# A seventh seven-product pair in the second column pair of the second MLP product

## The chip, the cores and the metric

The kernel runs on one core of a Trainium2 chip. The metric is device time in microseconds (us) of one execution of the whole program; a lower time is better. The kernel before takes 2110.73 us (median of three runs, 2110.59 to 2112.64).

## The reference

Four pre-norm residual layers share one residual stream `x` of 256 tokens by 2048 features, in fp32. Two of them mix tokens (one with latent attention and a matrix memory, one with dilated attention), and each of these is followed by a squared-ReLU MLP. The change concerns the two MLPs alone:

```python
D_MODEL = 2048; SEQ = 256; D_FF = 4 * D_MODEL

def squared_relu_mlp(h, w1, w2):
    return jnp.square(jax.nn.relu(h @ w1)) @ w2

# per layer
x = x + mix
x = x + squared_relu_mlp(rms_norm(x, norm_mlp[layer]), mlp_w1[layer], mlp_w2[layer])
# after the last
return rms_norm(x, norm_final)
```

The second product, `(256 x 8192) @ (8192 x 2048)`, is what the change is about.

## The kernel before

Every fp32 product is made from three products of rounded halves. A weight tile `wr` comes from memory (`load`, L127), ScalarE rounds it to the high half `wh` (L135), VectorE subtracts to get the low half `wl` (L136), and TensorE multiplies high by high, high by low and low by high (`mm_three`, L154 to L156, 512 columns each; `mm_feats`, L164 with 512 columns and L168 with 256).

**The MLP by quarters.** The 8192 hidden features are worked in four quarters of 2048, that is 16 blocks of 128 or 8 *K-pairs* of two blocks. For each quarter `q` the second product is added into `x` in two halves of the output columns, called column pairs: columns 0 to 1023 first, then 1024 to 2047. While the first column pair of quarter `q` is computed, the hidden blocks 8 to 15 of the same quarter are computed between its steps (`hs[NF // 2:]`); while the second column pair is computed, the hidden blocks 0 to 7 of the next quarter are (`hs[:NF // 2]`). `woven` puts the steps of the second product evenly before the blocks, and the rest of the steps follow behind the last block. The fourth quarter differs: its second column pair has three K-pairs of the first kind below, with no blocks between, and in the last layer it lies in `finish`, which also makes the final norm.

**Two ways to multiply a K-pair.** For a K-pair the operands are a 2 by 2 arrangement of blocks (two token blocks, two feature blocks) and weights (two feature blocks, two column chunks of 512).

- *Eight products* (`eight`): two steps, one for each column chunk, each with one weight tile of 128 x 1024, rounded and split. 8 products of three matmuls, 24 matmuls.
- *Seven products* (`steps_seven`, the inner `seven`): the weights' sums `ta` (L224) and `tb` (L225, L226) are made on VectorE from two loads `r0` and `r1`, and seven products of three matmuls, 21 matmuls, go to seven accumulators, the four banks `ym` and three banks `yc`. The step is cut into `go_a` (loads, sums, splits, three products) and `go_b` (four products). Load `r1` goes into a buffer `rb` of which there is one. After the last such pair, `early_y` combines the four `ym` banks on VectorE through two scratch tiles `yp` and `yq` and adds them to `x`; after the last `eight`, `late_y` (L1086) adds the `yc` banks.

A K-pair whose weights go by seven products needs its hidden activations as sums as well: the tile `pt`, made in `evac_h` from `hp` (L1051 to L1058). Activations of other pairs are split plainly into `ht`. An `eight` can read either (`operand`). The constant `SEVEN = 6` says how many of the 8 K-pairs get a `pt` (the buffer count of `pt` is `SEVEN`, that of `ht` is `2 * (NF // 2 - SEVEN)`), and both column pairs of the first three quarters, and the first of the fourth, run `range(SEVEN)` by seven products.

The accumulators of a hidden block come out through ScalarE into a scratch tile `bt_h` (L1037, two buffers of 128 x 512), are added on VectorE into `hu` (L1039), and go on from there. In `finish` the three pieces `gf` of the final gain are loaded by GpSimd's queue at its start (L957), two of them into the buffers of `bt`.

The Tile framework schedules the program: the order of each engine's instructions is fixed when the kernel is built, from program order and a model of when operands are ready, and may differ from the order of the source. Each engine works through its queue in that order.

Of the kernel before, what the change touches and what calls it, by code (L numbers as in the profile page):

```python
# [9 lines left out]
F32 = mybir.dt.float32  # L10
# [4 lines left out]
P = 128  # L15
# [3 lines left out]
KD = D // P  # L19
FF = 8192  # L20
NQ = 4
SEVEN = 6
EPS = 1e-6
BIG = -3.0e38
MLA_SCALE = 192 ** -0.5
# [44 lines left out]
def trunk(ctx: ExitStack, tc: tile.TileContext, plan, a, c_first, c_even, c_odd, out):  # L70
# [361 lines left out]
    def weave(main, side):  # L432

        done = 0
        for i, go in enumerate(main):
            go()
            want = (i + 1) * len(side) // max(1, len(main))
            while done < want:
                side[done]()
                done += 1  # L440
        for go in side[done:]:
            go()
# [509 lines left out]
    def finish(H, wq, early, scale, sm):  # L952

        gfs = []
        for i, (o, n, tag, bufs) in enumerate(((0, 1024, "hp", 1), (1024, 512, "bt", 2), (1536, 512, "bt", 2))):
            g = sm.tile([P, n], F32, name=f"gf{i}", tag=tag, bufs=bufs)
            nc.gpsimd.dma_start(g, a["norm_final"][o:o + n].rearrange("(o d) -> o d", o=1).to_broadcast([P, n]))  # L957
            gfs.append((o, n, g))

        def gf(lo, hi):  # L960
            return next(g[:, lo - o:hi - o] for o, n, g in gfs if o <= lo < o + n)
# [20 lines left out]
        hold = [NF // 2 - 2, NF // 2 - 1]  # L982
        box = {}
        seven, eight = steps_seven(sm, H, [0, 1, 2], wq, 1024, early, box.update, hold=hold)
        weave(sum([a + b for a, b in zip(seven, eight)], []), [gain(0), gain(1)])
        w = {(k, j): weights(wq, 2 * k, 2, 1024 + 512 * j, 512) for j in range(2) for k in hold}
        for b in range(NB):
            pieces = [(0, 0, 512), (1, 0, 512)] if b == 0 else [(0, 0, 512), (1, 0, 256), (1, 256, 512)]
# [35 lines left out]
    def mlp(layer, norm, nxt):  # L1024
# [38 lines left out]
        def early_y(c):  # L1063
            def go(m1, m5, m6, m7):
                def add(b, j, src):
                    v = x[b][c + j]
                    nc.vector.scalar_tensor_tensor(v, src, scale["s"][:, b:b + 1], v, OP.mult, OP.add)

                p = sm.tile([P, 512], F32, name="yp", tag="yp", bufs=1)
                q = sm.tile([P, 512], F32, name="yq", tag="yq", bufs=1)  # L1070
                nc.scalar.activation(p, m1, AF.Copy)
                add(0, 0, m1)
                nc.vector.tensor_add(p, m6, p)
                nc.vector.tensor_add(q, m7, p)
                nc.vector.tensor_sub(p, m5, p)
                add(1, 0, q)
                nc.vector.tensor_sub(q, m5, q)
                add(0, 1, p)
                add(1, 1, q)
            return go  # L1080
# [21 lines left out]
        H = [None] * NF  # L1102
# [9 lines left out]
        for q in range(NQ):  # L1112
            last = q == NQ - 1
            wq = ("mlp_w2", layer, q * (FF // NQ))
            seven, eight = steps_seven(sm, H, list(range(SEVEN)), wq, 0, early_y(0), late_y(0))
            woven(hs[NF // 2:], sum(seven, []))
            run(*eight)
            if last and nxt is None:
                finish(H, wq, early_y(2), scale, sm)
                break  # L1120
            pairs = list(range(3 if last else SEVEN))
            seven, eight = steps_seven(sm, H, pairs, wq, 1024, early_y(2), late_y(2))
            if last:
                nxt.stats(0)
                nxt.stats(1)
                steps = sum([a + b for a, b in zip(seven, eight)] + eight[len(seven):], [])
                run(steps[:-1], [lambda: nxt.turn(0)], steps[-1:], [lambda: nxt.turn(1)])
                break
            H = [None] * NF
            hs, _ = blocks(q + 1, H)  # L1130
            sv = sum(seven, [])
            woven(hs[:NF // 2], sv)
            run(*eight)
# [67 lines left out]
```

## Time and profile before

| | us |
|---|---|
| median of three runs | 2110.73 (2110.59 to 2112.64) |
| profiled execution | 2109.76 |
| its span, first to last instruction | 2108.0 |
| TensorE busy | 2089.8 (99%) |
| VectorE busy | 1742.3 (83%) |
| ScalarE busy | 1302.0 (62%) |
| granted TensorE clock | 0.999 of full speed |

Each row of a timeline is one instruction (or a run of equal ones, `x8`): its start from the span's start, its duration, the engine, the line of the kernel, the operation and its operands. Matmuls overlap in the pipeline, so the pace of TensorE is read from start to start and not from the durations (0.39 us for 512 columns); the same holds to a smaller degree of VectorE.

In the first MLP, the stretch from 486.86 us to 570.99 us is the second column pair of the first quarter, the one from 570.99 us to about 655.1 us the first column pair of the second quarter, and so on in turns.

### The profile page before, as it was taken

The numbers are of one execution on the slowest core, as the hardware profiler recorded it, in microseconds if no ns is written. First come the engines' busy times: TensorE is split into PE (matmuls) and PEld (weight loads), VectorE is DVE, ScalarE is ACT, GpSimd is POOL, SyncE is SP. The second block draws the span as 40 slices with busy tenths as digits, with TensorE's granted clock in tenths as the row PEclk, the third lists the DMA queues.
The fourth block names the chain that finished last, engine by engine and source line by source line (L and its number), as shares of the span: only waits on it lengthen the run. The fifth ranks groups of instructions, "written<-read, shape, count | busy, mean of one in ns | idle before, by whom it ended". The sixth has DMA issues, their size and how long they took to land.

```text
span 2108.0 us, 29391 instructions
## 1 busy us (share of the span) xinstructions
PE 2089.8 (99%) x10860; PEld 1798.0 (85%) x10860; DVE 1742.3 (83%) x2455; ACT 1302.0 (62%) x1876; POOL 6.1 (0%) x13
## 2 busy tenths in 40 slices
PE   8999999999999999999999999999999999999998
PEld 8998888888888888888888888888888888888887
DVE  5678555889999999999877667557999999999988
ACT  6576445766666766666544544457766666666665
POOL 0000000000000000000000000000000000000000
PEclk9999999999999999999999999999999999999999
DMA  8554455566566566565555555455665665656664
GB/s 295 164 176 156 160 179 194 176 200 213 184 203 209 195 200 205 191 209 192 188 193 177 169 178 173 160 190 180 200 209 192 196 206 196 212 190 198 208 208 153
DMA packets 115296, 404.51 MB, mean 192 GB/s; under 512 B 12944, under 2 KB 13584, under 8 KB 115152
## 3 DMA queue, kind: packets, MB, share of 16 engines
q1 hardware_dynamic: 114048, 400.02, 57.9%
q8 instruction: 85, 1.39, 0.3%
q0 software_dynamic: 384, 1.51, 0.3%
q10 hardware_dynamic: 720, 1.11, 0.1%
q14 instruction: 59, 0.48, 0.1%
HBM read 400.49 MB, written 2.10 MB: 191 GB/s over the span
## 4 chain that ended last, share of the span: by engine, by line
PE 93%; DVE 3%; DMA 2%; issue 1%; ACT 1%; SPq 0%; POOLq 0%; POOL 0%; DVEq 0%; ACTq 0%
PE h L164 21%; PE h L168 11%; PE yc L154 6%; PE yc L155 6%; PE yc L156 6%; PE ym L155 4%; PE ym L154 4%; PE ym L156 4%; PE k L164 3%; PE o L154 3%; PE o L156 3%; PE o L155 3%; PE q L164 3%; PE v L154 2%; PE v L156 2%; PE v L155 2%
## 5 line engine op out<-in xcount | busy, mean ns | idle before, releaser
L136 DVE TENSOR_TENSOR wl<-wr,wh 128x1024 fp32r<-128x1024 f32 (+4 forms) x769 | 864.7, 1133 | 257.2 <-ACT wh L135 251.9
L135 ACT ACTIVATE wh<-wr 128x1024 fp32r<-128x1024 f32 (+4 forms) x769 | 753.9, 986 | 523.1 <-PE h L164 149.6
L164 PE MATMUL h<-T,wh 128*128 128x512 f32 x2048 | 511.3, 392 | 0.5 <-ACT wh L135 0.4
L164 PEld LDWEIGHTS h<-T,wh 128*128 128x128 f32 x2048 | 374.5, 188 | 75.1 <-ACT wh L135 2.5
L168 PEld LDWEIGHTS h<-T,wl 128*128 128x128 f32 x2048 | 279.3, 190 | 20.1
L168 PE MATMUL h<-T,wl 128*128 128x256 f32 x2048 | 285.5, 282 | 0.0
L155 PE MATMUL ym<-wl,pt 128*128 128x512 f32 x360 | 141.2, 392 | 0.7 <-DVE wl L136 0.7
L156 PE MATMUL ym<-wh,pt 128*128 128x512 f32 x360 | 140.1, 389 | 0.0
L154 PE MATMUL ym<-wh,pt 128*128 128x512 f32 x360 | 139.1, 392 | 0.0
L224 DVE TENSOR_TENSOR ta<-wr,wr 128x1024 f32<-128x1024 f32 x90 | 109.9, 1222 | 29.9 <-DMA wr<-in_mlp_w 28.5
L135 ACT ACTIVATE wh<-ta 128x1024 fp32r<-128x1024 f32 x90 | 95.1, 1056 | 61.5 <-DVE ta L224 61.3
L155 PE MATMUL yc<-wl,pt 128*128 128x512 f32 x318 | 123.9, 390 | 0.0
L154 PE MATMUL yc<-wh,pt 128*128 128x512 f32 x318 | 123.1, 390 | 0.0
L156 PE MATMUL yc<-wh,pt 128*128 128x512 f32 x318 | 122.7, 389 | 0.0
L1040 ACT ACTIVATE hu<-hu 128x256 f32<-128x256 f32 x128 | 52.7, 415 | 104.3 <-DVE hu L1039 104.2
L136 DVE TENSOR_TENSOR wl<-tb,wh 128x1024 fp32r<-128x1024 f32 x90 | 109.6, 1218 | 1.1 <-ACT wh L135 1.1
L135 ACT ACTIVATE wh<-tb 128x1024 fp32r<-128x1024 f32 x90 | 94.5, 1050 | 24.8 <-DVE tb L226 24.5
L136 DVE TENSOR_TENSOR wl<-ta,wh 128x1024 fp32r<-128x1024 f32 x90 | 109.6, 1217 | 0.0
L154 PE MATMUL o<-wh,M 128*128 128x512 f32 x256 | 102.3, 400 | 0.0
L156 PE MATMUL o<-wh,M 128*128 128x512 f32 x256 | 99.8, 390 | 0.0
L155 PE MATMUL o<-wl,M 128*128 128x512 f32 x256 | 99.6, 389 | 0.0
L154 PE MATMUL yc<-wh,ht 128*128 128x512 f32 (+1 forms) x256 | 99.4, 388 | 0.0
(297 smaller groups left out, 3318.8 us busy)
## 6 DMA issues: line engine op xcount, KB each, us to landing
wr<-in_mlp_w SPq DMA_DIRECT2D x512, 512.0 KB, 4.2
wr<-in_od_w_qkv SPq DMA_DIRECT2D x96, 512.0 KB, 3.9
wr<-in_ev_w_in SPq DMA_DIRECT2D x32, 512.0 KB, 3.5
wr<-in_ev_w_out SPq DMA_DIRECT2D x32, 512.0 KB, 3.4
wr<-in_od_w_out SPq DMA_DIRECT2D x32, 512.0 KB, 3.4
wr<-in_ev_w_in SPq DMA_DIRECT2D x24, 344.0 KB, 3.2
wr<-in_ev_w_in SPq DMA_DIRECT2D x15, 364.0 KB, 5.9
wr<-in_mla_w_ukv SPq DMA_DIRECT2D x8, 512.0 KB, 3.8
```

What stands on the lines that cost most here:

```text
L135: nc.scalar.activation(hi, raw, AF.Copy)
L136: nc.vector.tensor_tensor(lo, raw, hi.bitcast(F32), OP.subtract)
L154: nc.tensor.matmul(ac, xh, hi, start=first, stop=False)
L155: nc.tensor.matmul(ac, xh, lo, start=False, stop=False)
L156: nc.tensor.matmul(ac, xl, hi, start=False, stop=last)
L164: nc.tensor.matmul(acs[f], hi[:, j, f * P:(f + 1) * P], Ts[j].rearrange("p a t -> p (a t)"), start=first and j == 0, stop=False)
L168: nc.tensor.matmul(acs[f][:, :S], lo[:, j, f * P:(f + 1) * P], Ts[j][:, 0, :], start=False, stop=last and j == n - 1)
L224: nc.vector.tensor_tensor(ta, r0, r1[:, 0:1, :].to_broadcast([P, 2, 512]), OP.add)
L1040: nc.scalar.activation(u, u, AF.Relu)
```

## The change

`SEVEN` becomes 7. The first column pair is given `range(SEVEN - 1)`, so it still runs six K-pairs by seven products and two by eight; the second column pair of the first three quarters runs `range(SEVEN)`, so seven K-pairs go by seven products and one by eight. The fourth quarter's second column pair is left at three. Seven `pt` tiles are kept instead of six, and two `ht` tiles instead of four; the activations of K-pair 6 are now made as a `pt` in every quarter. `yp` and `yq` lose their own buffers and share the two buffers of `bt` with `bt_h`. In `finish` the two gain pieces that live in `bt` are loaded behind the woven steps instead of at the start.

```diff
-SEVEN = 6
+SEVEN = 7
@@ finish
-        for i, (o, n, tag, bufs) in enumerate(((0, 1024, "hp", 1), (1024, 512, "bt", 2), (1536, 512, "bt", 2))):
-            g = sm.tile([P, n], F32, name=f"gf{i}", tag=tag, bufs=bufs)
+        def gain_tile(o, n, tag, bufs):
+            g = sm.tile([P, n], F32, name=f"gf{o}", tag=tag, bufs=bufs)
             nc.gpsimd.dma_start(g, a["norm_final"][o:o + n].rearrange("(o d) -> o d", o=1).to_broadcast([P, n]))
             gfs.append((o, n, g))
+        gain_tile(0, 1024, "hp", 1)
...
-        weave(sum([a + b for a, b in zip(seven, eight)], []), [gain(0), gain(1)])
+        weave(sum([s + e for s, e in zip(seven, eight)], []), [gain(0), gain(1)])
+        gain_tile(1024, 512, "bt", 2)
+        gain_tile(1536, 512, "bt", 2)
@@ early_y
-                p = sm.tile([P, 512], F32, name="yp", tag="yp", bufs=1)
-                q = sm.tile([P, 512], F32, name="yq", tag="yq", bufs=1)
+                p = sm.tile([P, 512], F32, name="yp", tag="bt", bufs=2)
+                q = sm.tile([P, 512], F32, name="yq", tag="bt", bufs=2)
@@ mlp, for q in range(NQ)
-            seven, eight = steps_seven(sm, H, list(range(SEVEN)), wq, 0, early_y(0), late_y(0))
+            seven, eight = steps_seven(sm, H, list(range(SEVEN - 1)), wq, 0, early_y(0), late_y(0))
```

## Rows read from the trace of the kernel before

**Rows 1.** Page, part 1: busy time of each engine, share of the span, instructions.
```profile
PE 2089.8 (99%) x10860; PEld 1798.0 (85%) x10860; DVE 1742.3 (83%) x2455; ACT 1302.0 (62%) x1876; POOL 6.1 (0%) x13
```

**Rows 2.** Busy time by stretch: length, PE, PEld, DVE, ACT, POOL, clock, DMA.
```profile
487.00:571.00 84.00, 84.00 (x432) 71.80 (x431) 79.11 (x98) 56.38 (x73) 0.00 (x0) 1.00 0.59 197
571.00:655.00 84.00, 84.00 (x431) 71.90 (x430) 78.53 (x96) 55.51 (x75) 0.00 (x0) 1.00 0.62 203
2049.40:2092.20 42.80, 42.80 (x191) 35.38 (x190) 42.77 (x50) 24.23 (x32) 0.00 (x0) 1.00 0.55 177
```

**Rows 3.** Waits over the whole span: who for whom, total us, times, longest.
```profile
ACT wh L135 <- PE h L164: 149.6, 139, 2.1
...
PE ym L155 <- DVE wl L136: 0.7, 1, 0.7
```

**Rows 4.** Timeline of PE: a seven-product pair begins, the block behind it begins.
```profile
486.86 0.39 PE L154 MATMUL ym<-wh,pt 128*128 128x512 f32 x1
...
491.62 0.62 PE L164 MATMUL h<-T,wh 128*128 128x512 f32 x2
```

**Rows 5.** Timeline of PE: a hidden block begins, the step behind it begins.
```profile
575.75 1.98 PE L164 MATMUL h<-T,wh 128*128 128x512 f32 x8
...
581.31 0.40 PE L154 MATMUL ym<-wh,pt 128*128 128x512 f32 x1
```

**Rows 6.** Timeline of DVE: three instructions back to back.
```profile
541.82 1.22 DVE L136 TENSOR_TENSOR wl<-tb,wh 128x1024 fp32r<-128x1024 f32 x1
542.96 0.69 DVE L136 TENSOR_TENSOR wl<-wr,wh 128x512 fp32r<-128x512 f32 x1
543.56 0.42 DVE L1039 TENSOR_TENSOR hu<-bt_h 128x256 f32<-128x256 f32 x1
```

**Rows 7.** Groups of DVE by line: busy us, mean ns, idle before.
```profile
L1058 DVE TENSOR_TENSOR pt<-hp,pt 128x1024 fp32r<-128x1024 f32 x48 | 58.6, 1221 | 0.2
...
L1053 DVE TENSOR_TENSOR hp<-hp 128x256 f32<-128x256 f32 x48 | 20.1, 420 | 7.5 <-ACT hp L1051 7.5
```

**Rows 8.** Waits of DVE in the second column pair, 487 to 571 us.
```profile
DVE wl L136 <- ACT wh L135: 2.6, 3, 0.9
DVE ta L224 <- DMA wr<-in_mlp_w: 0.9, 2, 0.8
DVE hp L1053 <- ACT hp L1051: 0.9, 1, 0.9
```

**Rows 9.** Waits of DVE in the first column pair, 571 to 655 us.
```profile
DVE wl L136 <- ACT wh L135: 2.6, 4, 1.1
DVE ta L224 <- DMA wr<-in_mlp_w: 2.5, 2, 1.5
```

**Rows 10.** Timeline of DVE at the start of a first column pair.
```profile
571.86 1.22 DVE L136 TENSOR_TENSOR wl<-ta,wh 128x1024 fp32r<-128x1024 f32 x1
```

**Rows 11.** Timeline of PE there: first matmul, first with the low half of `ta`.
```profile
570.99 0.39 PE L154 MATMUL ym<-wh,pt 128*128 128x512 f32 x1
...
573.49 0.39 PE L155 MATMUL ym<-wl,pt 128*128 128x512 f32 x1
```

**Rows 12.** Timelines of DVE and ACT: last read of `yp`, next `bt_h`.
```profile
556.31 0.74 DVE L1067 SCALAR_TENSOR_TENSOR x<-yp,iv_mlp,x 128x512 f32<-128x512 f32 x1
...
560.30 0.58 ACT L1037 ACTIVATE bt_h<-h 128x512 f32<-128x512 f32 x1
```

**Rows 13.** Timeline of DVE in `finish`: last reads of `yp` and `yq`, first use of `gf`'s second piece.
```profile
2086.15 0.74 DVE L1067 SCALAR_TENSOR_TENSOR x<-yp,iv_mlp,x 128x512 f32<-128x512 f32 x1
...
2088.54 0.74 DVE L1067 SCALAR_TENSOR_TENSOR x<-yq,iv_mlp,x 128x512 f32<-128x512 f32 x1
...
2093.09 0.69 DVE L1005 TENSOR_TENSOR x<-x,gf 128x512 f32<-128x512 f32 x1
```

**Rows 14.** DMA issues: KB each, median us to landing.
```profile
gf<-in_norm_final POOLq DMA_DIRECT2D x2, 256.0 KB, 4.8
```

**Rows 15.** Timeline of DVE: a `ta` that waits for its load.
```profile
611.32 1.23 DVE L224 TENSOR_TENSOR ta<-wr,wr 128x1024 f32<-128x1024 f32 x1 [1.50 <-DMA wr<-in_mlp_w]
```

## The prediction

> **What bounds the kernel now.** I read the busy times of the page first: TensorE is busy for 99% of the span, VectorE for 83% [rows 1]. A share over the span hides the stage, so I next read the busy times of single stretches of the MLP. In the second column pair of a quarter TensorE is busy for all of 84.0 us and VectorE for 79.1 of them; in the first column pair VectorE has 78.5 [rows 2]. TensorE sets the time there, and VectorE is 94% full. The list of waits says the same: over the whole span TensorE stood only once for a low half in a seven-product step, for 0.7 us [rows 3]. Last I read the timelines at the seams of the stretches, to see how far ahead VectorE is. At the start of a first column pair the low half of `ta` is done at 571.86 + 1.22 = 573.08 us and is used at 573.49 us [rows 10, 11]: 0.41 us to spare. There is hardly a lead at the seams. So two limits lie close together, and the question is whether work can be moved from TensorE to VectorE here.
>
> **What TensorE is spared.** A seven-product pair takes from 486.86 to 491.62 us, 4.76 us for 21 matmuls, 0.227 us each [rows 4]. An eight-product pair has 24 of them, 5.44 us. One K-pair is changed in each of three quarters of two layers, so six times 3 x 0.227 = 0.68 us, in all 18 matmuls and 4.08 us. TensorE is without gaps there, so this is the most that the change can bring: 0.19% of 2110.73 us. The Trainium skill, page "TensorE: Matmul & The Clock Gate", section "Back-to-back issue gap", gives about 131 ns as the sustained spacing of 512-column matmuls in a stream with weight loads; by that 18 matmuls would be only 2.4 us. The row of this kernel says 227 ns, and the row decides.
>
> **What VectorE is given, second column pair.** Instructions back to back start 1.14 us apart for 1024 columns and 0.60 us for 512 [rows 6]. A seven-product pair has four of the first kind (`ta` and the low halves of `r0`, `ta`, `tb`) and three of the second (two for `tb`, the low half of one half of `r1`): 6.36 us. An eight-product pair has two of 1024: 2.28 us. So each of the six stretches gets 4.1 us more, 79.1 + 4.1 = 83.2 us, while TensorE's time falls from 84.13 (486.86 to 570.99 us, [rows 4, 11]) to 83.45 us. Busy alone still fits, by 0.25 us. But VectorE also stands idle there: 2.6 us for `wh`, 0.9 us for a load and 0.9 us for `hp` [rows 8]. The 2.6 us I count as slack, since ScalarE's `wh` in turn mostly waits for TensorE to free a buffer [rows 3]: that wait goes when VectorE is late. The other 1.8 us I count as staying. Then VectorE needs 85.0 us in a stretch of 83.45 us: 1.55 us too much, six times.
>
> **First column pair.** K-pair 6 is now made as a `pt`: three subtractions of 256 and 128 columns and one of 1024 [rows 7] in place of two of 256 columns for `ht` (L302, of the form of L1053). That is 1.22 + 0.42 us, two of 128 columns between 0 and 0.42 us each, less 0.84 us: 0.8 to 1.6 us more, of which I take 1.2, as half a 256-column one is nearest. It happens once in each of eight quarters. VectorE then has 78.5 + 1.2 = 79.7 us of 84.13, and idles now for 2.6 us for `wh` and 2.5 us for loads [rows 9]. The first covers it, and it costs nothing. Without that cover it would be 1.2 us, eight times.
>
> **Both together.** 83.2 + 79.7 us of work, and 1.8 + 2.5 us of waits that I count as staying, are 167.2 us. TensorE needs 83.45 + 84.13 = 167.6 us for the same two stretches. So VectorE fits over two stretches, though not over the second column pair alone: whether TensorE stands depends on whether 1.55 us of lateness can be carried over the seam. I see a way to carry it. At the seam TensorE's order has already been changed: from 570.99 to 573.49 us it runs 11 matmuls that need no low half of `ta` or `tb` [rows 11]. The schedule is made with the readiness of operands in it, and behind these stand the next block's eight L164 matmuls, which need high halves alone, 8 x 0.227 = 1.8 us. With 0.41 us there already, 1.14 us would have to be filled, and 1.8 us are to hand. The finish also shows VectorE busy for 42.77 of 42.80 us with TensorE never idle [rows 2], so a full VectorE doesn't by itself stop TensorE.
>
> **The price of what is not carried** lies between 0 (the finish) and 1.14 us per seam. The nearest row is the one stall seen, 0.7 us at one of the seven-product steps [rows 3]; I take half of it, 0.35 us, as the margin is used up at some steps and not at others: 6 x 0.35 = 2.1 us.
>
> **The other edits.** *Shared buffers.* `bt_h` of the last block now waits for `yp`. Today `yp` is last read at 556.31 + 0.74 = 557.05 us and that `bt_h` is written at 560.30 us [rows 12]: 3.2 us of cover, 1.7 us if VectorE is 1.55 us late. ScalarE's roundings stand behind a waiting `bt_h`, and VectorE behind them. I take nothing. *Gain pieces.* They now load behind `yp` and `yq`: the first can go at 2086.89 us and needs 4.8 us [rows 13, 14], so it lands at about 2091.7 us, for a use at 2093.09 us. If it gets the buffer of `yq`, free at 2089.28 us, it lands at 2094.1 us and VectorE's final additions are up to 1 us late. GpSimd's queue holds nothing else between them but the small power of the norm. I take nothing. *Loads.* The bytes are the same; both ways move two tiles of 512 KB.
>
> **The sum.** The profiled execution took 2109.76 us (span 2108.0 and 1.76 around it). Less 4.08, plus 2.1, it would be 2107.8 us. The median of the runs is 0.97 us above that execution, so the forecast is 2108.7 us, 0.1% below 2110.73. A measurement of this kernel can tell about 0.2%, 4.2 us, from no change, and the forecast lies inside.
>
> **Rivals.** *A, VectorE becomes the bound and TensorE pays at each seam (slower).* The seven-product steps now follow each other every 4.76 + 5.56 = 10.3 us (a pair and a block, [rows 4, 5]). `r1` has one buffer: its next load can't be issued before the low half of the last one is made. Where the steps are as dense as that today, `ta` waits 1.50 us for its load [rows 15], and VectorE, which takes its queue in order, stands with it. If the load waits of such a stretch are the first column pair's 2.5 us instead of 0.9, and nothing is carried over the seam, TensorE stands 1.14 + 1.6 = 2.7 us, six times 16.4 us, less 4.1: 2123 us. The point from which it decides: a stall of more than 0.68 + 0.70 = 1.4 us per seam makes the kernel slower by over 0.2%. Its middle, 2.1 us, gives 2119 us. For it speak the margins at the seams; against it, that the schedule fills them with other matmuls. The Trainium skill, page "TensorE: Matmul & The Clock Gate", in its part on engine queue depths, calls VectorE's queue a strict FIFO, which would make each such wait hold up all that stands behind it; the idle time ahead of that `ta` agrees. *B, the shared buffers stop ScalarE (slower).* If VectorE is more than 3.2 us late with `early_y`, ScalarE waits for the rest; at 5 us it is 1.8 us in each of the 14 stretches that have a block behind `early_y`, 25 us: 2134 us. Nothing in the rows is that late. *C, all of it is won (faster or equal).* No stall at all gives 2106.65 us, 0.14 us short of the bound; any small gain, as the 0.9 us of `hp` being filled, or the scatter between runs, puts it past that.
>
> **Chances.** The forecast 0.50; A 0.30; B 0.06; C 0.14, which I count as faster. So faster 0.14, within 0.2% 0.50, slower 0.36. The range: C at its lower end, some 0.5 us of scatter under it, 2106.2, up to the upper part of A, 2121; what lies above (the end of A, and B) and below is under 2 in 10. The likeliest case alone spans 2106.65 to 2113.5 us, the latter with 1.14 us at every seam.
>
> **What will show it.** Right: 18 matmuls fewer; second column pairs with 103 VectorE instructions and over 83 us of them busy; idle for `wh` nearly gone there; L164 matmuls moved ahead of low-half ones at the seams; stalls of TensorE on `wl` under 0.5 us each. Wrong toward A: stretches of 85 us and more, with TensorE waiting for `wl` behind a `ta` that waits for its load. Wrong toward B: ScalarE waiting at L1037 for L1067. If `gf` waits appear in front of L1005, the finish is to blame.

## The result and the profile after

The changed kernel takes 2121.9 us (median of four runs, 2120.2 to 2123.8), the kernel before 2110.7 us beside it (2109.7 to 2112.6). The ratio is 1.0053, with a 95% interval of 1.0041 to 1.0065: 11.3 us slower. The forecast was 2108.7 us in a range of 2106.2 to 2121.0, so the time lies above the range and the sign is the other one. The profiled execution took 2122.43 us, with a span of 2120.6 us.

The first part of the page of the changed kernel (it answers to [rows 1]), then the chain of work that ended last, by engine, of the kernel before and of the changed one:

```profile
PE 2097.3 (99%) x10842; PEld 1790.8 (84%) x10842; DVE 1774.3 (84%) x2501; ACT 1311.4 (62%) x1880; POOL 6.1 (0%) x13
...
PE 93%; DVE 3%; DMA 2%; issue 1%; ACT 1%; SPq 0%; POOLq 0%; POOL 0%; DVEq 0%; ACTq 0%
...
PE 83%; DVE 10%; DMA 4%; issue 2%; ACT 1%; SPq 0%; DVEq 0%; POOLq 0%; POOL 0%; ACTq 0%
```

TensorE has 18 matmuls fewer than in [rows 1], as it should. Yet it is still "busy" for 99% of the longer span: the busy time of a matmul that had to wait includes part of the wait (0.50 us in a row further down, instead of 0.39). The share of busy time doesn't show the loss here. VectorE's share of the chain, 10% instead of 3%, and the lengths of the stretches do. Next the busy times of one second column pair and of the first column pair behind it, in the changed kernel, cut where the first `ym` matmul of each stretch starts (length, then PE, PEld, DVE, ACT, POOL, clock, DMA; they answer to [rows 2]):

```profile
486.76:570.84 84.08, 83.96 (x428) 71.23 (x427) 79.26 (x97) 55.82 (x73) 0.00 (x0) 1.00 0.60 194
570.84:657.55 86.71, 85.83 (x432) 71.36 (x430) 83.73 (x104) 57.95 (x76) 0.00 (x0) 1.00 0.62 201
```

The second column pair, where a K-pair was changed, takes 84.08 us; in the six of them it is 83.5 to 84.1 us, at or under the 84.13 us of before. The first column pair *behind* it, where TensorE's work is unchanged, takes 86.71 us instead of 84.13; in the six it is 86.5 to 87.4 us (84.1 to 85.4 before). Added up, the six second column pairs are 2.4 us shorter than before, and the six first column pairs behind them 14.4 us longer. So nearly the whole loss lies in the first column pairs that follow a changed stretch. VectorE has 79.26 + 83.73 = 163.0 us of work in the two stretches; 83.2 + 79.7 = 162.9 were forecast, but with the larger part in the first of the two. Some 4 us of VectorE's work have slid over the seam (97 instructions in the second column pair, where 103 were expected).

The waits of TensorE, then one of ScalarE, over the whole span of the changed kernel (who for whom: total us, times, longest; they answer to [rows 3]):

```profile
PE ym L154 <- ACT wh L135: 2.0, 6, 0.3
PE h L164 <- ACT bt_h L1042: 1.4, 3, 0.6
PE h L164 <- DVE x L1091: 1.3, 6, 0.2
...
ACT bt_h L1042 <- DVE x L1072: 5.6, 6, 1.2
```

They come three to six times, at the seams of the six changed quarters or up to 15 us behind them. The last one is the shared buffers: ScalarE can't evacuate a hidden block until `early_y` has read its scratch tile. It is there six times, and up to 1.2 us long; before, `bt_h` waited for nothing of the kind. Next the seam of [rows 10 to 12]: the kernel before (ScalarE, TensorE, VectorE), the changed kernel's ScalarE and VectorE in order of time, then its TensorE:

```profile
547.63 0.58 ACT L1071 ACTIVATE yp<-ym 128x512 f32<-128x512 f32 x1
...
554.53 1.98 PE L164 MATMUL h<-T,wh 128*128 128x512 f32 x8
...
563.44 1.22 DVE L224 TENSOR_TENSOR ta<-wr,wr 128x1024 f32<-128x1024 f32 x1
```

```profile
557.28 0.58 ACT L1042 ACTIVATE bt_h<-h 128x512 f32<-128x512 f32 x1
557.76 0.59 ACT L1076 ACTIVATE yp<-ym 128x512 f32<-128x512 f32 x1
558.89 0.75 DVE L1072 SCALAR_TENSOR_TENSOR x<-ym,iv_mlp,x 128x512 f32<-128x512 f32 x1
...
561.05 1.23 DVE L224 TENSOR_TENSOR ta<-wr,wr 128x1024 f32<-128x1024 f32 x1 [0.82 <-DMA wr<-in_mlp_w]
...
565.19 0.74 DVE L1072 SCALAR_TENSOR_TENSOR x<-yp,iv_mlp,x 128x512 f32<-128x512 f32 x1
...
566.03 0.60 ACT L1042 ACTIVATE bt_h<-h 128x512 f32<-128x512 f32 x1 [0.77 <-DVE x L1072]
```

```profile
559.81 1.98 PE L164 MATMUL h<-T,wh 128*128 128x512 f32 x8
...
572.59 2.08 PE L164 MATMUL h<-T,wh 128*128 128x512 f32 x8 [0.22 <-DVE x L1091]
...
577.24 0.50 PE L154 MATMUL ym<-wh,pt 128*128 128x512 f32 x1 [0.34 <-ACT wh L135]
...
579.63 1.16 PE L168 MATMUL h<-T,wl 128*128 128x256 f32 x8
...
585.00 1.20 PE L164 MATMUL h<-T,wh 128*128 128x512 f32 x4 [0.25 <-ACT bt_h L1042]
```

The hidden block behind the last seven-product step starts at 559.81 us, 554.53 us before (its first L164 matmul), and is due to be evacuated 5.8 us after its start (560.30 - 554.53). The last read of `yp` ends 2.5 us after that start before (557.05 us, [rows 12]) and 6.1 us after it in the changed kernel; in the six it is 6.1 to 6.9 us. So VectorE is 3.6 to 4.4 us late with `early_y`, measured from the step that `early_y` follows. The rows show two things that make it late. First, ScalarE's copy into `yp`, with which `early_y` begins, now takes its turn in the buffers of `bt` and runs behind the `bt_h` of the block ahead: 2.1 us before the block's start instead of 6.9. With it the first addition of `early_y` (558.89 us, 0.66 us to the next start) has moved from 5 us ahead of the block to 0.9 us ahead of it, into the stretch that VectorE works through without any slack. Second, the next pair's `ta` stands among the operations of `early_y` and waits 0.82 us for its load, 0.8 to 1.6 us at the six seams; before, it came behind `early_y` and didn't wait.

The eight L164 matmuls are indeed moved ahead (572.59 us), but they stop too, for the PSUM bank that `late_y` still reads; then the next high half is late, and a block's evacuation behind it. ScalarE's own wait for `yp` is a sign of VectorE's lateness and not a cause of it: from that `ta` to 8 us behind the seam the profile shows no idle time of VectorE, at any of the six seams, and at this one ScalarE waits 2.07 us for VectorE right behind that `bt_h`.

### The profile page after: what moved, and what is told of

Read it like the earlier page. It is cut to its first block, busy times and chain, and to the rows that moved or that the text cites. A ratio compares the mean times of both kernels' runs of the same rounds, so it can differ in the third digit from the quotient of the medians.

```text
span 2120.6 us, 29384 instructions
## 1 busy us (share of the span) xinstructions
PE 2097.3 (99%) x10842; PEld 1790.8 (84%) x10842; DVE 1774.3 (84%) x2501; ACT 1311.4 (62%) x1880; POOL 6.1 (0%) x13
## 4 chain that ended last, share of the span: by engine, by line
PE 83%; DVE 10%; DMA 4%; issue 2%; ACT 1%; SPq 0%; DVEq 0%; POOLq 0%; POOL 0%; ACTq 0%
PE h L164 19%; PE h L168 10%; DVE wl L136 5%; PE yc L156 4%; PE yc L155 4%; PE yc L154 4%; PE ym L155 3%; PE ym L156 3%; PE ym L154 3%; DMA wr<-in_mlp_w 3%; PE k L164 3%; PE o L154 3%; PE o L156 3%; PE o L155 3%; PE q L164 3%; PE v L154 2%
## 5 line engine op out<-in xcount | busy, mean ns | idle before, releaser
L164 PE MATMUL h<-T,wh 128*128 128x512 f32 x2048 | 514.3, 392 | 3.5 <-ACT bt_h L1042 1.4
L164 PEld LDWEIGHTS h<-T,wh 128*128 128x128 f32 x2048 | 373.2, 188 | 83.6 <-ACT wh L135 6.4
L168 PEld LDWEIGHTS h<-T,wl 128*128 128x128 f32 x2048 | 278.9, 190 | 20.8 <-DVE wl L136 1.2
L168 PE MATMUL h<-T,wl 128*128 128x256 f32 x2048 | 285.7, 282 | 0.0
L155 PE MATMUL yc<-wl,pt 128*128 128x512 f32 x416 | 162.7, 391 | 0.5
L154 PE MATMUL yc<-wh,pt 128*128 128x512 f32 x416 | 160.6, 391 | 0.8 <-DVE x L1091 0.7
L156 PE MATMUL yc<-wh,pt 128*128 128x512 f32 x416 | 160.4, 389 | 0.0
L155 PE MATMUL ym<-wl,pt 128*128 128x512 f32 x384 | 151.4, 394 | 0.0
L156 PE MATMUL ym<-wh,pt 128*128 128x512 f32 x384 | 149.6, 390 | 0.0
L154 PE MATMUL ym<-wh,pt 128*128 128x512 f32 x384 | 147.1, 393 | 2.0 <-ACT wh L135 2.0
L224 DVE TENSOR_TENSOR ta<-wr,wr 128x1024 f32<-128x1024 f32 x96 | 117.2, 1221 | 23.2 <-DMA wr<-in_mlp_w 22.1
L135 ACT ACTIVATE wh<-ta 128x1024 fp32r<-128x1024 f32 x96 | 101.3, 1055 | 49.8 <-DVE ta L224 49.7
L136 DVE TENSOR_TENSOR wl<-tb,wh 128x1024 fp32r<-128x1024 f32 x96 | 116.9, 1218 | 1.1 <-ACT wh L135 1.1
L136 DVE TENSOR_TENSOR wl<-ta,wh 128x1024 fp32r<-128x1024 f32 x96 | 116.9, 1218 | 0.0
L135 ACT ACTIVATE wh<-tb 128x1024 fp32r<-128x1024 f32 x96 | 101.2, 1054 | 25.0 <-DVE tb L226 24.1
L155 PEld LDWEIGHTS yc<-wl,pt 128*128 128x128 f32 x416 | 78.1, 188 | 19.0 <-DVE wl L136 3.1
```

The costliest lines, as they stand in the source:

```text
L135: nc.scalar.activation(hi, raw, AF.Copy)
L136: nc.vector.tensor_tensor(lo, raw, hi.bitcast(F32), OP.subtract)
L154: nc.tensor.matmul(ac, xh, hi, start=first, stop=False)
L155: nc.tensor.matmul(ac, xh, lo, start=False, stop=False)
L156: nc.tensor.matmul(ac, xl, hi, start=False, stop=last)
L164: nc.tensor.matmul(acs[f], hi[:, j, f * P:(f + 1) * P], Ts[j].rearrange("p a t -> p (a t)"), start=first and j == 0, stop=False)
```

## The experiments

Three theories of the 11.3 + 4.1 = 15.4 us that TensorE stands were set against each other: T1, VectorE's load (4.1 us more per second column pair, 1.55 more than it has time for); T2, the parts besides the seventh pair (scratch tiles in the buffers of `bt`, the `pt` of K-pair 6 in the first column pairs); T3, the tail: behind the last seven-product step lie now one hidden block and one `eight`, 5.56 + 5.44 = 11.0 us ([rows 4, 5]), where two of them made 16.4. Differences are of medians within one set of runs, the version and the kernel before beside each other on one chip; the half-width of their 95% intervals is 1.8 to 3.6 us.

### The parts besides the seventh pair

*The kernel before with the shared buffers and the moved gain pieces alone:*

```diff
-                p = sm.tile([P, 512], F32, name="yp", tag="yp", bufs=1)
-                q = sm.tile([P, 512], F32, name="yq", tag="yq", bufs=1)
+                p = sm.tile([P, 512], F32, name="yp", tag="bt", bufs=2)
+                q = sm.tile([P, 512], F32, name="yq", tag="bt", bufs=2)
```

> The kernel before with only the buffers changed: yp and yq share bt with bt_h, and the two gain pieces load behind the woven steps. It tells what part of the 3 us of e1 is the buffers'. If the shared buffers hold ScalarE up, 2112 to 2114 us; if K-pair 6's form is the cause, 2109.8 us within 1 us.

2112.9 against 2110.5 us: +2.4 (ratio 1.0003 to 1.0022). In this order, with `early_y` behind the sixth pair, the sharing costs little. No `bt_h` waits for `yp` here, but the copy into `yp` is late here too, by 4.8 us, and at the seam of [rows 10] the low half of `ta` is 0.6 us later.

*The changed kernel with six seven-product pairs in the second column pair again:*

```diff
-            pairs = list(range(3 if last else SEVEN))
+            pairs = list(range(3 if last else SEVEN - 1))
```

> The changed kernel with the second column pair back at six seven-product pairs; K-pair 6 is still made as a pt, and yp and yq still share bt's buffers. Theory 1, VectorE's load by the seventh pair (4.1 us in each of six second column pairs) makes it late at the seam: without that load 2110.7 us, the time of the kernel before, within 1.5 us. Theory 2, the shared buffers and K-pair 6's longer preparation hold ScalarE and VectorE up: most of the loss stays, 2118 us or more. Theory 3, the shorter tail (one eight-product pair in place of two behind the last seven-product pair) leaves early_y and late_y too little time, whatever VectorE's load: 2110.7 us.

2113.0 against 2109.8 us: +3.2 (1.0004 to 1.0023). What is left of it beside the sharing's 2.4 is less than the interval.

*The changed kernel with the scratch tiles elsewhere:* one tile in the buffer of `ta`, the gain pieces loaded at the start as before.

```diff
-                p = sm.tile([P, 512], F32, name="yp", tag="bt", bufs=2)
-                q = sm.tile([P, 512], F32, name="yq", tag="bt", bufs=2)
+                pq = sm.tile([P, 2, 512], F32, name="yp", tag="ta", bufs=1)
+                p, q = pq[:, 0, :], pq[:, 1, :]
```

> The changed kernel, but the scratch tiles of early_y lie in one tile that takes the buffer of ta instead of the two buffers of bt, and the gain pieces are loaded at the start of finish as before; everything is computed. ScalarE's evacuation of a block then no longer waits for early_y, but the first ta of the next column pair does. If the shared buffers have a part of their own in the changed kernel, as the kernel before with nothing but the sharing showed (+2.4 us), this run is 2.4 to 5 us under the changed kernel's 2121.9: 2117 to 2119.5. If the sharing only takes over a wait that VectorE's lateness would cause in any case, or if the wait of ta for early_y costs as much, it stays at 2121 to 2123. In the waits ScalarE's bt_h behind L1072 (5.6 us) must be gone in either case.

2113.3 against 2109.9 us: +3.3 (1.0008 to 1.0026). That is 8 us less than the changed kernel, more than any expectation. The stretches of [rows 2] in this kernel, and the end of `early_y` and the evacuation beside it:

```profile
486.65:570.12 83.47, 83.47 (x429) 71.38 (x428) 80.25 (x98) 56.78 (x74) 0.00 (x0) 1.00 0.60 192
570.12:655.48 85.36, 85.36 (x432) 71.57 (x431) 83.17 (x103) 57.08 (x76) 0.00 (x0) 1.00 0.64 206
```

```profile
552.17 0.57 ACT L1076 ACTIVATE yp<-ym 128x512 f32<-128x512 f32 x1
...
559.09 1.98 PE L164 MATMUL h<-T,wh 128*128 128x512 f32 x8
...
563.26 0.74 DVE L1072 SCALAR_TENSOR_TENSOR x<-yp,iv_mlp,x 128x512 f32<-128x512 f32 x1
...
564.85 0.60 ACT L1042 ACTIVATE bt_h<-h 128x512 f32<-128x512 f32 x1 [0.32 <-PE h L168]
565.06 1.22 DVE L224 TENSOR_TENSOR ta<-wr,wr 128x1024 f32<-128x1024 f32 x1
```

`bt_h` waits for the block alone. The edit changes the order as well: the copy into `yp` runs 6.9 us before the block's start again, and `ta`, which needs the buffer of `yp` now, comes behind `early_y` and waits for no load. The second column pair takes 83.47 us, the forecast's 83.45; the first takes 85.36, so 1.2 us are still lost behind the seam. The 1.35 us between the two kernels at this seam (86.71 and 85.36) are about what VectorE is spared around the last seven-product step: the addition that had moved, 0.66 us, and 0.65 us of standing (0.82 for the load, less 0.17 that it stands here). Over the six, the first column pairs take 85.5 us in the mean, 86.9 with the sharing: six times the 1.4 us are about the 8 us.

*Controls: the same scratch in the kernel before, and in the kernel with six seven-product pairs again.*

> The kernel before with nothing but the scratch tiles of early_y in one tile in the buffer of ta. The control of the runs with that edit: if the place of the scratch tiles costs nothing there, it gives what the kernel before gives, within 1 us (2109 to 2111). If the next ta waits for early_y, or the serial use of one tile costs, it is 2 us and more above (2112 to 2114), and the 3.3 us by which the changed kernel with this edit is slower than before is then in part due to it.

> The changed kernel with the second column pair back at six seven-product pairs and the scratch tiles in the buffer of ta: of the change, only the pt of the seventh pair is left, some 1.2 us of VectorE work more in each first column pair. If that is hidden, as predicted, this equals the control with the same scratch, within 1 us. If it is not, it lies 2 to 7 us above (up to 1.2 us in each of the six stretches behind which a second column pair follows), and part of the cost of the changed kernel lies in the first column pairs.

2110.4 and 2110.0 against 2110.1 us: +0.2 and -0.1 (0.9993 to 1.0011, 0.9994 to 1.0012). The place in `ta` costs nothing, and the `pt` of K-pair 6 is hidden in the first column pairs, which take 84.13 us at this seam, with VectorE at 80.14, and no longer than before at the others:

```profile
571.35:655.48 84.13, 84.13 (x431) 72.00 (x430) 80.14 (x98) 56.18 (x74) 0.00 (x0) 1.00 0.63 204
```

### VectorE's load

*The kernel before with 4.6 us more VectorE work* in the sixth pair of the six second column pairs (`ta`, `tb` and their low halves made twice):

```diff
-                nc.vector.tensor_tensor(ta, r0, r1[:, 0:1, :].to_broadcast([P, 2, 512]), OP.add)
...
+                for _ in range(2 if k in twice else 1):
+                    nc.vector.tensor_tensor(ta, r0, r1[:, 0:1, :].to_broadcast([P, 2, 512]), OP.add)
...
+                if k in twice:
+                    nc.vector.tensor_tensor(l1, ta, h1.bitcast(F32), OP.subtract)
+                    nc.vector.tensor_tensor(t[2][1], tb, t[2][0].bitcast(F32), OP.subtract)
```

> The kernel before, with VectorE making the sums and the two low halves of the sixth pair twice in the second column pair of the first three quarters: 4.6 us more VectorE work in each of six stretches, nothing else. Theory 1: VectorE then has 83.7 us of 84.1 and idles that stay, so TensorE stands 2 to 3 us per seam: 2122 to 2129 us. Theories 2 and 3: buffers and tail are those of before, 2110.7 us within 2 us.

2122.6 against 2109.8 us: +12.7 (1.0039 to 1.0073), 2.1 us for each of the six. The budget of the prediction was right in kind: 4.6 us more per second column pair are not to be had for nothing.

*The changed kernel without the seventh pair's sums,* 4.6 us of VectorE's work less per stretch:

```diff
+                if k in plain:
+                    t[0] = h0, l0 = halves(r0)
+                    t[3] = halves(r1[:, 1:2, :])
...
+                    nc.scalar.activation(h1, r0, AF.Copy)
+                    nc.scalar.activation(h2, r0, AF.Copy)
...
-            seven, eight = steps_seven(sm, H, pairs, wq, 1024, early_y(2), late_y(2))
+            seven, eight = steps_seven(sm, H, pairs, wq, 1024, early_y(2), late_y(2), plain=(6,))
```

> The changed kernel, but the seventh pair of the second column pair leaves out the weights' sums and their low halves (ta, tb and two subtractions, 4.6 us of VectorE each time); ScalarE's roundings, the loads and all 21 matmuls stay, on rounded copies of r0, so that the product of that pair is another one. Theory 1: VectorE is back at 78.6 us in these stretches and the whole 4.08 us of TensorE show: 2106.6 us, up to 2108. Theory 2: the buffers and the preparation are unchanged, 2119 to 2122 us. Theory 3: the tail is as short as in the changed kernel, 2115 to 2122 us.

2117.0 against 2109.8 us: +7.2 (1.002 to 1.0044), 4 us less than the changed kernel. The scratch is still in `bt` and the copy into `yp` as late as in the changed kernel, but no `bt_h` waits for `early_y`, and `ta` waits at most 0.2 us for its load at the seams.

### The tail

*The kernel before without one `eight`* in each of the six stretches (K-pair 6 left out, its loads kept): nothing shared, no seventh pair, the tail 11.0 us long.

```diff
-        rest = [k for k in range(len(H) // 2) if k not in pairs and k not in hold]
+        rest = [k for k in range(len(H) // 2) if k not in pairs and k not in hold and k not in skip]
```

> The kernel before, leaving out the eight-product pair 6 of the second column pair in the first three quarters (its loads stay, its rounding, splitting and 24 matmuls go): TensorE has 5.44 us less in each of six stretches, VectorE 2.3 us less, and the tail behind the last seven-product pair is 11.0 us, as in the changed kernel. Theory 1: VectorE has 76.8 us of 78.7 and keeps up: 2109.8 - 32.6 = 2077.2 us, up to 2079. Theory 3: the short tail alone makes TensorE stand at the seam, 1.5 to 2.5 us each as in e4: 2086 to 2092 us.

2083.1 against 2110.5 us: -27.5 (0.9857 to 0.9884). Six times 5.44 are 32.6 us, so 5.2 are given back, and the stretches say where:

```profile
487.11:566.09 78.98, 78.98 (x408) 67.36 (x407) 73.18 (x90) 51.89 (x70) 0.00 (x0) 1.00 0.59 204
566.09:652.12 86.03, 85.78 (x432) 71.37 (x430) 82.45 (x102) 57.39 (x77) 0.00 (x0) 1.00 0.62 206
```

The shortened stretch has nearly all of its 5.44 us (six times 78.7 to 79.2 us); the one behind it is 1.2 to 2.1 us longer than 84.13 (up to 1.2 before). That is less than the 1.5 to 2.5 us per seam of the expectation. VectorE has less work here than before, not more. A shorter tail alone makes TensorE stand.

*The changed kernel with two hidden blocks behind the last seven-product step* (tail 16.6 us):

```diff
-            woven(hs[:NF // 2], sv)
+            woven(hs[:NF // 2 - 1], sv)
+            run(hs[NF // 2 - 1:NF // 2])
```

> The changed kernel, but in the second column pair all fourteen half steps of the seven pairs stand before the last two blocks instead of before the last one, so that 5.56 + 5.56 + 5.44 = 16.6 us of TensorE lie behind the last seven-product pair, as in the kernel before (5.56 + 2 x 5.44 = 16.4), instead of 11.0. Nothing else changes, and VectorE's work is the same. Theory 3, the tail is too short for what VectorE has to do in it (early_y, late_y, the next pair's sums): the waits at the seam go, and what is left is the 4.08 us won and e1's 3 us: 2107 to 2111 us. Theory 1, VectorE's total in the stretch: 2118 to 2122 us, as changed.

2116.3 against 2110.5 us: +5.8 (1.0019 to 1.004), 5.6 us less than the changed kernel, and between the two expectations.

### All together

Every combination of the three edits was run: scratch in `bt` or in `ta`, sums made or left out, one block or two in the tail.

> The changed kernel with two edits at once: the scratch tiles of early_y in the buffer of ta (as in the run before this one), and the order with two blocks behind the last seven-product step of a second column pair instead of one, which alone gave 2116.3. Everything is computed. If the shared buffers and the short tail are two causes that add up, it gives 2116.3 less 2.4 to 5, so 2111 to 2114, and what is left over 2106.6 is VectorE's load. If both remove the same standing, it stays at 2115 to 2117. Faster than the kernel before would mean that VectorE's load costs less than the 4.08 us won.

> The changed kernel with the seventh pair's weight sums ta and tb left out (part of the computation: its products take plain halves of the weights), 4.6 us of VectorE work less in each of the six stretches, and two blocks behind the last seven-product step. The shared buffers stay. If VectorE's load and the short tail are separate causes, the sum is 2121.9 - 4.9 - 5.6 = 2111.4 us or less, and down to 2109 if only the sharing's 2.4 us are left over 2106.6. If the tail costs only because VectorE is late, it stays near the better of the two, 2115 to 2117.

> All three at once: the seventh pair's sums left out (part of the computation), two blocks behind the last seven-product step, and the scratch tiles of early_y in the buffer of ta. If VectorE's load, the short tail and the shared buffers are the whole account of the 15.4 us that TensorE stands, all of the 4.08 us is won and this gives 2106.5 to 2107.5 us. A fourth cause shows as what lies above that: 2110 us or more would say that at least 3.5 us of the account are still without a name.

> The changed kernel with the scratch tiles of early_y in the buffer of ta, without the seventh pair's weight sums (part of the computation), and with its own order of one block behind the last seven-product step. If VectorE's load and the shared buffers are the whole account and the short tail is no cause of its own, all of the 4.08 us is won: 2105.8 to 2107 us against 2109.9, which is under the 2107.8 of the same kernel with two blocks behind. If the short tail costs something by itself, as the theory of three causes had it, this lies above that one: 2109 to 2111.

Difference to the kernel before, us (4.1 won without any standing would be -4.1):

| scratch, sums | one block behind | two blocks behind |
|---|---|---|
| in `bt`, sums made | +11.3 (the change) | +5.8 |
| in `bt`, sums left out | +7.2 | -1.1 |
| in `ta`, sums made | +3.3 | +5.6 |
| in `ta`, sums left out | +3.2 | -2.1 |

The expectation that the causes add up failed. With one block and the scratch in `ta`, leaving out the sums gains nothing (+3.3, +3.2), where one theory expected all of the 4.1 us and the other 2109 to 2111 us; 2113.3 lies above both. With sums, the second block doesn't help once the sharing is gone (+5.6). Only with both mended is most of the gain there. (The last 2 us lie in the second column pairs: in the profile of that kernel they take 83.7 us in four of six and 84.3 and 84.8 in two, 3.4 us over six times 83.45, where the kernel before has 0.7 us over six times 84.13.) That is the picture of two limits, one behind the other, of which the later one sets the time.

*The sharing.* Without the sums and with one block, the sharing still costs 4.0 us (+7.2 against +3.2), 0.67 us per seam, though no `bt_h` waits for `early_y` there. That is the size of the addition that has moved, 0.66 us. With two blocks the copy into `yp` comes at about the same point in both layouts (without the sums, VectorE's order behind it is the same too), and the sharing costs 0.2 to 1.0 us, less than the intervals. So the traces put the cost of the sharing down to what it moves into VectorE's tail, its work around and behind the last seven-product step. No run changes the place of that addition, or of `ta`, alone.

*The tail's limit.* The kernel with scratch in `ta` and no sums, one block; its stretches, then VectorE and TensorE behind the seam:

```profile
486.54:570.07 83.53, 83.53 (x428) 71.31 (x427) 75.93 (x93) 56.88 (x74) 0.00 (x0) 1.00 0.60 192
570.07:655.42 85.35, 85.35 (x431) 71.55 (x430) 83.11 (x103) 57.03 (x76) 0.00 (x0) 1.00 0.63 206
```

```profile
574.19 1.22 DVE L136 TENSOR_TENSOR wl<-ta,wh 128x1024 fp32r<-128x1024 f32 x1
575.33 1.22 DVE L136 TENSOR_TENSOR wl<-tb,wh 128x1024 fp32r<-128x1024 f32 x1
576.46 2.35 DVE L136 TENSOR_TENSOR wl<-wr,wh 128x1024 fp32r<-128x1024 f32 x2
```

```profile
576.60 0.50 PE L155 MATMUL ym<-wl,pt 128*128 128x512 f32 x1
...
577.74 1.22 PE L168 MATMUL h<-T,wl 128*128 128x256 f32 x8
```

VectorE has 75.93 + 83.11 = 159.0 us of work in two stretches in which TensorE has 167.6, and still the second of them takes 85.35 us, the same as with the sums. TensorE starts a low-half step at 576.60 us, right when `wl` of `tb` ends (575.33 + 1.22), and L168 at 577.74, right behind the next low halves: it walks behind VectorE. Nearly all of VectorE's work for the seam (`early_y` from its second accumulator on, `late_y`, and behind them in its queue the next pair's sums and halves) can't begin until the last seven-product step is nearly done, so the sums, which lie ahead of that, don't matter, nor does idle time there. From that step on VectorE should be late by what the tail lost, as an estimate from the rows: 5.44 us of TensorE's time, which held 2.28 us of VectorE's work, so 3.2 us; less 0.41 to spare and 1.8 by the L164 matmuls is 0.95. Measured: 1.2. At four or five of the six seams TensorE stops at the same places, 1.0 to 1.2 us in all, with the sums, without them, and in the kernel before without one `eight`. With two blocks in the tail the same kernel has it no more:

```profile
486.50:570.23 83.73, 83.73 (x428) 71.29 (x427) 77.40 (x96) 56.93 (x74) 0.00 (x0) 1.00 0.61 201
570.23:654.36 84.13, 84.13 (x431) 71.99 (x430) 80.75 (x100) 57.10 (x75) 0.00 (x0) 1.00 0.63 201
```

*The limit by load.* With two blocks, the sums cost 7.7 us (+5.6 against -2.1) or 6.9 (+5.8 against -1.1): 1.15 to 1.3 us per stretch, in the first column pairs again, and now with TensorE waiting for `wl` at the first `ym` step: behind all six seams with the scratch in `bt`, behind two of them with the scratch in `ta` (its third wait lies in the last column pair). The waits of these two kernels, then one stretch of the second:

```profile
PE ym L155 <- DVE wl L136: 3.8, 6, 0.9
...
PE ym L155 <- DVE wl L136: 1.4, 3, 0.6
```

```profile
740.02:826.16 86.14, 85.37 (x431) 71.70 (x430) 82.10 (x102) 57.50 (x76) 0.00 (x0) 1.00 0.63 199
```

### VectorE's work on GpSimd

*Three versions that were to relieve VectorE:* the four subtractions for `pt` on GpSimd; the largest of them alone (its low half, 128 x 1024); and, with the scratch in `ta`, only the first sum of the seventh pair, six operations in all.

```diff
-                nc.vector.tensor_tensor(ta, r0, r1[:, 0:1, :].to_broadcast([P, 2, 512]), OP.add)
+                (nc.gpsimd if k == 6 else nc.vector).tensor_tensor(ta, r0, r1[:, 0:1, :].to_broadcast([P, 2, 512]), OP.add)
```

> The changed kernel with the four subtractions that make a pt (L1058 to L1060 and L1063) on GpSimd instead of VectorE: 1.9 us less for VectorE per pt, four of them in each stretch, 7.5 us. Theory 1: VectorE has slack again and the 4.08 us show, 2106.6 us, if GpSimd keeps pace and doesn't slow VectorE down; if it slows VectorE, up to 2120 us. Theory 2: the buffers are still shared, so 2115 us or more. Theory 3: the tail is unchanged, 2115 us or more.

> The changed kernel with only the low half of pt (L1063) on GpSimd, so that no ScalarE instruction waits for GpSimd (in e6 those waits were 140 us). VectorE is relieved of 4 x 1.14 = 4.6 us in each stretch, one of them in the tail. Theory 1: as e4, 2117 us, and less if e4's other waits were VectorE's. Theory 3: 2115 to 2119 us, the tail is relieved of 1.1 us of some 5. If GpSimd slows VectorE by the 7% that e6's subtractions show, 4 x 2.4 us x 7% a stretch is too little to see.

> The changed kernel with the scratch tiles in the buffer of ta, and the first of the seventh pair's three weight sums (ta, 128 x 1024) made on GpSimd instead of VectorE; everything is computed. VectorE is spared 1.14 us in each of the six stretches, nearly the 1.2 us by which it costs TensorE there. If that is all that counts, six times about 1 us are won on 2113.3: 2107 to 2108, under the kernel before. Against it: GpSimd's own 128 x 1024 operation took 2.4 to 4.5 us in the runs with work on GpSimd, and VectorE's operations beside it took 7 to 14% longer, some 0.4 us of each 1.14 us given back, and the low half of ta is made that much later, so 2111 to 2114.

2280.1 us (+170; 1.0788 to 1.082), 2163.3 (+53; 1.0233 to 1.0261) and 2130.9 (+21; 1.0081 to 1.0107). The last is the telling one. Its one kind of operation on GpSimd, the longest new wait of VectorE, one such wait, and TensorE beside it:

```profile
L224 POOL TENSOR_TENSOR ta<-wr,wr 128x1024 f32<-128x1024 f32 x6 | 14.3, 2390 | 1727.3 <-DMA wr<-in_mlp_w 1727.3
```

```profile
DVE tb L225 <- POOL ta L224: 17.7, 6, 3.0
```

```profile
544.88 0.69 DVE L225 TENSOR_TENSOR tb<-ta,wr 128x512 f32<-128x512 f32 x1 [2.90 <-POOL ta L224]
```

```profile
552.54 2.11 PE L164 MATMUL h<-T,wh 128*128 128x512 f32 x8 [1.80 <-ACT wh L135]
```

Saving VectorE 1.14 us makes it stand for 2.9 us: `tb` is next in its queue and needs the sum, and what stands behind `tb`, which doesn't, stands too. The rounding of `ta` is late as well, and TensorE stops for 1.8 us, once in each of the six stretches (86 us each instead of 83.5). The expected 0.4 us for slower operations were the smaller matter.

## Why the prediction was wrong

*What held.* TensorE was spared 18 matmuls, and where nothing else stood in the way the second column pair fell to 83.47 us, against 83.45 in the sum. VectorE's work was sized right: 163.0 us for two stretches against 162.9. That VectorE can't do 4.1 us more in a second column pair showed in the run with extra work alone (2.1 us per stretch) and in the sums' 1.15 to 1.3 us per stretch with the long tail, near the 1.55 us that were counted. The `pt` in the first column pairs is hidden. VectorE doesn't wait for the gain pieces in the finish. Rival A was right in its direction, and the time is at its upper part. Its mechanism, a `ta` that waits for its load and holds up VectorE's queue, is there too, but at the six seams (0.8 to 1.6 us each, none there before) and not over whole stretches: over the span `ta` waited 22.1 us for loads, 28.5 before.

*The step on the shared buffers failed, and was the larger part: 8 us taken as nothing.* It asked one question, whether `bt_h` has to wait for `yp`, and took VectorE to be at most 1.55 us late, against a cover of 3.2 us. VectorE was 3.6 to 4.4 us late with `early_y`, so the cover was gone. That is the condition of Rival B, more than 3.2 us, which got 0.06; but the wait that it priced is not what costs the time. The other side of the sharing was left out: `yp` must take its turn behind `bt_h`, so that `early_y` begins later, and the next `ta` comes among its operations and waits for its load. That puts about 0.66 us of work and 0.65 us of standing into VectorE's tail at a seam, where the two places of the scratch differ by 1.35 us. The sharing alone costs 2.4 us in the kernel before and 4.0 us without the sums, with no `bt_h` waiting for `yp` in either, and 0.2 to 1.0 us with two blocks behind.

*The step on the price per seam failed: 0.35 us taken, 1.2 us measured,* at the upper end (1.14) of its own bounds: 7.4 us for six seams where 2.1 were taken. The 1.8 us of L164 matmuls were moved ahead, as foreseen, but lateness was counted over the whole stretch, and it arises in the tail, the stretch behind the last seven-product step. There the change takes 5.44 us of TensorE's time away and 2.28 us of VectorE's, a balance of 3.2 us against the 0.41 that were to spare, and the 4.76 us that TensorE gets in exchange lie ahead of the point at which VectorE's tail work can begin. The finish, taken as evidence that a full VectorE needn't stop TensorE, has no such seam.

*The sum with the measured terms:* 2109.76 - 4.08 + 7.4 + 8 + 0.97 = 2122 us; measured were 2121.9. That it agrees proves nothing, since the 7.4 and the 8 us are differences of the same runs; and since the causes don't add in general (the table), this is the account of this order of steps alone.

*What stays open.* How the sharing costs 2.4 us in the kernel before wasn't settled: the low half of `ta` is 0.6 us later at the seams, but the profile shows its stops, single ones of 1.3 to 1.7 us, at other places. Why the load of `ta` is late at the seams of the changed kernel is open, too, and the shares of the moved addition and of that wait in the 8 us are read from traces, not tested one by one. No version with the seventh pair that computes everything was faster than the kernel before; the nearest, with the scratch in `ta`, is 3.3 us slower.

## What to carry to other kernels

When a step is moved from one side of a dependency to the other, budget the stretch between the point where the dependent work can begin and the point where it is due, not the whole stretch: time won ahead of that point doesn't pay for work behind it. When two tiles are to share a buffer, ask on both sides who will wait: the old tile for the last read of the new one, and the new one for its turn behind the old; and read the cover from the order that the change makes. Where two limits lie one behind the other, taking away one of them shows nothing, so try the combinations before calling a cause harmless.

## What the runs showed of the hardware

GpSimd took 2.39 us for a 128 x 1024 sum in fp32, where VectorE takes 1.22. The times of both differed from version to version when GpSimd had more to do. The groups of the version with only the low half of `pt` on GpSimd (busy us, mean ns, idle before), then VectorE's `ta` in the changed kernel:

```profile
L1063 POOL TENSOR_TENSOR pt<-hp,pt 128x1024 fp32r<-128x1024 f32 x56 | 249.4, 4454 | 1709.0 <-ACT pt L1062 1651.2 <-issue 57.8
...
L224 DVE TENSOR_TENSOR ta<-wr,wr 128x1024 f32<-128x1024 f32 x96 | 131.6, 1371 | 38.2 <-DMA wr<-in_mlp_w 35.4 <-issue 1.7 <-DVE hu L1044 0.4
```

```profile
L224 DVE TENSOR_TENSOR ta<-wr,wr 128x1024 f32<-128x1024 f32 x96 | 117.2, 1221 | 23.2 <-DMA wr<-in_mlp_w 22.1 <-DVE hu L1044 0.7
```

This subtraction takes GpSimd 4.45 us in the mean here (half of them under 2.8 us, the longest 12.0), with VectorE busy for 83% of the span; in the version with all four subtractions on GpSimd it took 2.44, with VectorE at 78%. VectorE's own sums took 1371 ns in the mean here, instead of 1221: of its 908 sums and subtractions of 128 x 1024, 47 took over 1.4 us, all of them while GpSimd's subtraction ran, and none of 964 in the changed kernel. Spans on GpSimd are rough, and why GpSimd's own time differs between the two versions wasn't settled. The Trainium skill, page "GPSIMD Engine Reference", section "Specifications", says that GpSimd shares its SBUF interfaces with VectorE, with contention against VectorE instructions that have two SBUF inputs; these sums have two, and the rows agree.

Not expected either: a stop of TensorE costs more than the wait. In the kernel with scratch in `ta` and no sums, behind the seam:

```profile
574.19 0.86 PE L164 MATMUL h<-T,wh 128*128 128x512 f32 x3
575.04 0.50 PE L154 MATMUL ym<-wh,pt 128*128 128x512 f32 x1
575.38 0.40 PE L154 MATMUL yc<-wh,pt 128*128 128x512 f32 x1
575.61 0.39 PE L155 MATMUL ym<-wl,pt 128*128 128x512 f32 x1
```

The three L164 matmuls take 0.85 us from start to start, 0.17 over their pace of 0.227 each: the stop. The matmul behind the stop then takes 0.34 us to the next start, 0.11 over the pace. Between 574 and 594 us there are five such places, with 0.07 to 0.16 us each and 0.10 or 0.11 behind each. They make up 1.1 of the 1.2 us, and none is long enough to stand high in the list of waits.
